# A decoder block on one core: FFN weight sums issued two pieces ahead of their splits, and the first rest product in another pair of banks

## The chip, the cores and the metric

The kernel runs on one core of a Trainium2 chip. The metric is device time in microseconds of one execution, the median of several runs. Five engines matter: TensorE (PE, with its weight loads PEld), VectorE (DVE), ScalarE (ACT), GpSimd (POOL, which here only issues DMAs) and SyncE (SP, which issues most loads).

## The reference

One decoder layer in float32 over 512 positions of width 2048: latent attention and stick-breaking attention, merged by sigmoid gates, and then a SwiGLU FFN of inner width 5632. Cut to the part that the change touches:

```python
h2 = _rms(x, g_norm2) * (1 + sc2) + sh2
gate, up = jnp.split(h2 @ w_ffn_in, 2, axis=-1)
x = x + gt2 * ((jax.nn.silu(gate) * up) @ w_ffn_out)
```

`w_ffn_in` is 2048 x 11264, `w_ffn_out` 5632 x 2048.

## The kernel before, in words

All large products are float32 made out of three products of rounded halves: a weight `raw` is cast by ACT to a rounded `whi` and DVE subtracts, `wlo = raw - whi`; TensorE then does `wlo`·x-high, `whi`·x-high and `whi`·x-low. Three buffers of `whi` and three of `wlo` turn round.

The FFN is the last part. Its two matrices are cut in 2 x 2 blocks (11, 12, 21, 22) and multiplied with 7 block products in place of 8 (the Winograd scheme), P1 to P7, each of which takes a sum of blocks of the weights and a sum of blocks of the activations. The first matrix is worked through in 11 column groups (`FG`). In each, a product is 4 pieces (j0 to j3), a piece is one 128 x 1024 weight tile and 12 matmuls of 128 x 512. Activation sums are named `x12` and `x34` with h and l for the halves.

Groups 0 to 3 (`NPRE`) begin early: their products E1 and E2 (`ffn_in_early`) come first for all four, in banks ps_s for even groups and ps_t for odd ones, and ACT empties the banks afterwards (`out`). The rest of an early group is R5, R7, R3, R6, R4; a full group has P1, P5, P6, P3, P7, P2, P4 (`ffn_in_group`). The groups follow one another in the order 0, 4, 1, 5, 2, 6, 3, 7, 8, 9, 10 (`seq`). A product accumulates in a bank pair that has a letter: A is ps_s, ps_s; B is ps_t, ps_t; C is ps_mm, ps_mm; D is ps_mm, ps_y. R5 and R3 share B. After each group the result goes through transposes back to rows (`act_back1`, `act_back2`), is summed (`s12`, `s34`), split (`y12h`, `y12l`, `y34h`, `y34l`, and a plain `x22`) and parked in device memory (`apark`) by DMAs that POOL issues. `act_back2` of a group runs in the next one: after R5 in a rest group, after P1 in a full one. The second matrix (`ffn_out_chunk`) is worked through in five chunks of groups, its operands `yb` coming back from `apark`; each product is added to `acc` by DVE.

The weights: `raw_load` lets SP load a 128 x 1024 block into one of ten buffers (`raw2`). Where a product needs a sum of weight blocks, that sum is made in place by DVE, `raw <- raw + raw`: the tuple behind the product's name in `PROD`, for R7 `("12", "12", "22")`, says that block 12 becomes the sum of 12 and 22 (the minus signs of the scheme lie in the sums of activations). Only P7's is made by an accumulating DMA that POOL issues (`piece_add`). What sets the order: every product adds its pieces to a list (`add_piece`), other steps go between them (`add_do`), and `run_ev` goes through the list; for each piece `ahead_to(i, 2, 6)` first issues loads six pieces ahead and makes the splits two pieces ahead. `piece_make` issues for one piece: its sum if it has one, the cast `whi` on ACT, the `wlo` on DVE. Some steps wait in the list `late` and are let out two per piece (`flush(2)`). What comes out is the program order; the tile scheduler then orders each engine's instructions anew by when it expects them to be ready, so the places below are taken from the built kernels.

All vector operations are issued through a helper, so that the profile has one line for them: L83 before, L84 after.

Of the kernel before, what the change touches and what calls it, by code (L numbers as in the profile page):

```python
# [14 lines left out]
ALU = mybir.AluOpType  # L15
# [4 lines left out]
D = 2048  # L20
# [12 lines left out]
NF = 20  # L33
HSTEP = 2
GF = (1, 1)
NPRE = 4


# [50 lines left out]
def kernel(  # L89
# [22 lines left out]
    vec, act, pe = Ordered(tc, nc.vector), Ordered(tc, nc.scalar), Ordered(tc, nc.tensor)  # L112
# [13 lines left out]
    def nm(s):  # L126
        uid[0] += 1
        return f"{s}_{uid[0]}"

    def t2(name, dtype=F32, w=T):  # L130
        return tp.tile([P, w], dtype, tag="t2", name=nm(name))
# [8 lines left out]
    def ps(tag, w=T):  # L140
        return pp.tile([P, w], F32, tag=tag, name=nm("ps_" + tag), bufs=PSB[tag])
# [141 lines left out]
    for k in range(KD):  # L283
        t = t2("xt")
# [517 lines left out]
    for hh in range(H):  # L802
# [5 lines left out]
        last = hh == H - 1  # L808
# [336 lines left out]
    raws = {}  # L1145
# [16 lines left out]
    def raw_load(key):  # L1162
        if key in raws:
            return
        r = st["rp2"].tile([P, 1024], F32, tag="raw2", name=nm("raw2"))
        src, km = raw_src(key)
        sync_dma(r.rearrange("p (a b) -> p a b", b=128 if km else 256), src)
        raws[key] = r

    def raw_add(key, onto):  # L1170

        src, km = raw_src(key)
        nc.gpsimd.dma_start(raws[onto].rearrange("p (a b) -> p a b", b=128 if km else 256), src,  # L1173
                            accum_op=ALU.add)

    def kmc(key, ap):

        if key[0] == "a" and key[1] == 0:
            return ap.rearrange("p (k m c) -> p k m c", k=2, m=4)
        return ap.rearrange("p (m k c) -> p k m c", k=2, m=4)  # L1180
# [3 lines left out]
    PROD = {  # L1184
# [7 lines left out]

# [13 lines left out]
    def piece_add(stage, g, prod, j):  # L1206
        if prod == "P7":
            raw_add((stage, g, "22", j), (stage, g, "T3", j))

    def piece_make(stage, g, prod, j):  # L1210
        _, sums_, blk, _, last = PROD[prod]
        rw = lambda b: raws[stage, g, b, j]
        for d, x, y in sums_:
            vec.tensor_tensor(rw(d), rw(x), rw(y), ALU.add)
        key, r = (stage, g, blk, j), rw(blk)
        hi = wp.tile([P, 1024], F32R, tag="whi", name=nm("whi"), bufs=3)
        lo = wp.tile([P, 1024], F32R, tag="wlo", name=nm("wlo"), bufs=3)
        v4 = lambda t: t.rearrange("p (k m c) -> p k m c", k=2, m=4)
        act.copy(v4(hi), kmc(key, r))
        vec.tensor_tensor(v4(lo), kmc(key, r), v4(hi).bitcast(F32), ALU.subtract)  # L1220
        for b in last:
            del raws[stage, g, b, j]
        return hi, lo

    ev = []
    made = {}
    cur = {"load": 0, "add": 0, "make": 0}
    pieces = []

    def add_piece(args, use):  # L1230
        pieces.append(args)
        ev.append((len(pieces) - 1, use))
# [4 lines left out]
    def ahead_to(i, n_make, n_load):  # L1237
        while cur["load"] < min(i + n_load + 1, len(pieces)) or cur["make"] < min(i + n_make + 1, len(pieces)):
            if cur["load"] <= cur["make"] or cur["load"] < min(i + n_load + 1, len(pieces)):
                stage, g, prod, j = pieces[cur["load"]]  # L1240
                for b in PROD[prod][3]:
                    raw_load((stage, g, b, j))
                cur["load"] += 1
            else:
                while cur["add"] < min(cur["make"] + 4, cur["load"]):
                    piece_add(*pieces[cur["add"]])
                    cur["add"] += 1
                made[cur["make"]] = piece_make(*pieces[cur["make"]])
                cur["make"] += 1

    late = []

# [4 lines left out]
    def run_ev():  # L1257
        for i, fn in ev:
            if i is None:
                fn()  # L1260
            else:
                ahead_to(i, 2, 6)
                fn(made.pop(i))
                flush(2)

    def ffn_begin():
        ahead_to(0, 0, 3)

    def prod_mm(bank, hl, w, kk, first, last):

        wh, wl = w
        cs = slice(kk * 512, kk * 512 + 512)
        xh, xl = hl[:2]
        for t in range(2):
            mm3(bank[t], (xh[:, t * P:(t + 1) * P], xl[:, t * P:(t + 1) * P]), (wh[:, cs], wl[:, cs]),
                first, last, skip_group_check=True)

    def tb(*tags):
        return [ps(t) for t in tags]
# [25 lines left out]
    def ffn_in_group(g, early, prev):  # L1305
        G = groups.setdefault(g, {})
        n = KD // 4
# [6 lines left out]
        def product(prod, bank, start, stop, js=range(KD // 4)):  # L1314
            def use(w, j):
                if j == 0 and start:
                    G[bank] = tb(*{"A": ("s", "s"), "B": ("t", "t"), "C": ("mm", "mm"), "D": ("mm", "y")}[bank])
                for kk in range(2):
                    prod_mm(G[bank], X[PROD[prod][0], 2 * j + kk], w, kk, start and j == 0 and kk == 0,
                            stop and j == n - 1 and kk == 1)  # L1320
            for j in js:
                add_piece(("a", g, prod, j), lambda w, j=j: use(w, j))
# [81 lines left out]
        else:  # L1404
# [11 lines left out]
            if g == FG - 1:  # L1416
# [8 lines left out]
    epark = {(g, i, t): dp.tile([P, T], F32, name=f"epark_{g}_{i}_{t}")  # L1425
             for g in range(1, NPRE) for i in range(2) for t in range(2)}
    apark = [dp.tile([P, 7 * T], F32, name=f"apark_{i}") for i in range(2 * FG)]
# [87 lines left out]
    def mark_banks():  # L1515

        for o in tb("mm", "mm", "mm", "y"):
            pe.matmul(o, onesr, X[(1, 1), 0][2], start=True, stop=True)
    for g in range(0, NPRE, 2):
        for i in range(2):  # L1520
            ffn_in_early(g, i)
            ffn_in_early(g + 1, i)
    seq = [g for p in zip(range(NPRE), range(NPRE, 2 * NPRE)) for g in p] + list(range(2 * NPRE, FG))
    for g, prev in zip(seq, [None] + seq):
        ffn_in_group(g, g < NPRE, prev)

# [218 lines left out]
```

## Time and profile before

| | us |
|---|---|
| median of 3 runs | 2638.85 |
| lowest, highest | 2637.84, 2639.08 |
| the profiled execution | 2637.33 |
| its span, first to last instruction | 2635.6 |
| PE busy | 2568.4 (97%) |
| DVE busy | 1933.1 (73%) |
| ACT busy | 1176.8 (45%) |
| POOL busy | 221.5 (8%) |
| mean granted TensorE clock | 0.998 |

The profiled execution is a little below the median of the runs and 1.7 us longer than its own span. PE is busy nearly all the time, so an edit shows where PE was idle, or where its clock was low; idle time of the other engines costs nothing by itself. Times in the text are microseconds from the start of the span. The products of the FFN begin near 1307 us.

### The profile page before, as it was taken

The page shows a single profiled execution, that of the slowest core. Times are in us where ns is not written, and L with a number is a line of the kernel's source. Part 1 is how long each engine was busy: PE and PEld are TensorE (multiplying, and loading weights), DVE is VectorE, ACT ScalarE, POOL GpSimd, SP SyncE. Part 2 cuts the span into 40 slices and gives each one's busy share as a digit, 9 for nine tenths or more (in the row PEclk, how much of TensorE's full clock was granted, in tenths as well). Part 3 has the DMA queues.
Part 4 walks back from the last instruction along what each step waited for, and adds up shares of the span by engine and source line. Part 5 has one row for each costly group of instructions (what it writes and reads, how often), then busy time and mean ns, then how long its engine had stood idle before and what let it go on. Part 6 is the DMA issues. An engine that isn't in the chain of part 4 may idle for free. (4 is left out here: it accounts for less than half of the span.)

```text
span 2635.6 us, 32539 instructions
## 1 busy us (share of the span) xinstructions
PE 2568.4 (97%) x12170; PEld 2139.3 (81%) x12170; DVE 1933.1 (73%) x2507; ACT 1176.8 (45%) x1613; POOL 221.5 (8%) x316
## 2 busy tenths in 40 slices
PE   6999999999999999999999999999999999999998
PEld 4788887888998888888887878787888888788887
DVE  8967766666788764543587788887977778678887
ACT  4435556642333322222384545454555555444442
POOL 0000000000001100000000212121211221000001
PEclk9999999999999999999999999999999999999999
DMA  9864444435666695343475767675877778888894
GB/s 340 291 221 133 175 156 126 140 126 223 260 258 232 244 340 209 128 158 142 130 221 168 203 201 208 199 223 178 252 200 203 213 228 323 247 251 239 262 285 144
DMA packets 309477, 558.62 MB, mean 212 GB/s; under 512 B 17924, under 2 KB 229636, under 8 KB 284232
## 3 DMA queue, kind: packets, MB, share of 16 engines
q1 hardware_dynamic: 263424, 471.13, 52.5%
q0 software_dynamic: 39840, 74.73, 10.9%
q10 hardware_dynamic: 6056, 10.70, 1.1%
q8 instruction: 95, 1.56, 0.2%
q14 instruction: 62, 0.51, 0.1%
HBM read 494.09 MB, written 62.39 MB: 211 GB/s over the span
## 5 line engine op out<-in xcount | busy, mean ns | idle before, releaser
L83 ACT CAST whi<-raw 128x1024 fp32r<-128x1024 f32 x672 | 704.2, 1050 | 974.2 <-PE ps_mm L83 488.4
L83 DVE TENSOR_TENSOR wlo<-raw,whi 128x1024 fp32r<-128x1024 f32 x672 | 816.9, 1218 | 366.1 <-ACT whi L83 356.3
L83 PE MATMUL ps_mm<-hl,whi 128*128 128x512 f32 x832 | 327.2, 393 | 0.0
L83 PE MATMUL ps_mm<-hh,whi 128*128 128x512 f32 x832 | 325.0, 391 | 0.0
L83 PE MATMUL ps_mm<-hh,wlo 128*128 128x512 f32 x832 | 324.8, 390 | 0.0
L83 DVE TENSOR_TENSOR raw<-raw,raw 128x1024 f32<-128x1024 f32 x218 | 264.5, 1220 | 29.3 <-DMA raw<-in_w_ff_dram 26.8
L272 DVE CUSTOM_DVE_ANT_0 raw<-raw,cb,cols 128x2048 f32<-128x2048 f32 x96 | 224.6, 2344 | 4.5 <-DMA raw<-in_w_ada_dram 4.5
L83 PEld LDWEIGHTS ps_mm<-hh,wlo 128*128 128x128 f32 x832 | 156.2, 188 | 32.5
L83 PEld LDWEIGHTS ps_mm<-hl,whi 128*128 128x128 f32 x832 | 156.5, 188 | 30.5
L83 PEld LDWEIGHTS ps_mm<-hh,whi 128*128 128x128 f32 x832 | 156.5, 188 | 30.4
L83 PE MATMUL ps_s<-whi,x 128*128 128x512 f32 x576 | 177.6, 390 | 0.0
L83 PE MATMUL ps_mm<-whi,yb 128*128 128x512 f32 x440 | 135.6, 389 | 0.0
L83 PEld LDWEIGHTS ps_s<-whi,x 128*128 128x128 f32 x576 | 108.2, 188 | 22.6 <-DVE x L83 0.2
L83 PE MATMUL ps_s<-wlo,x 128*128 128x512 f32 x288 | 113.1, 393 | 1.8 <-ACT x L83 1.8
L83 PE MATMUL ps_mm<-whi,x 128*128 128x512 f32 x352 | 108.5, 389 | 0.0
L83 PE MATMUL ps_s<-whi,yb 128*128 128x512 f32 x352 | 108.5, 390 | 0.0
L83 PE MATMUL ps_t<-whi,yb 128*128 128x512 f32 x352 | 108.4, 389 | 0.0
L83 PE MATMUL ps_mm<-mgl,whi 128*128 128x512 f32 (+1 forms) x272 | 102.7, 377 | 0.0
L83 PE MATMUL ps_mm<-mgh,whi 128*128 128x512 f32 (+1 forms) x272 | 102.4, 376 | 0.0
L83 PE MATMUL ps_mm<-mgh,wlo 128*128 128x512 f32 (+1 forms) x272 | 102.4, 376 | 0.0
L1173 POOL DMA_DIRECT2D raw<-in_w_ff_dram x46 | 58.3, 1268 | 458.9 <-DMA raw<-in_w_ff_dram 236.3
L83 PEld LDWEIGHTS ps_mm<-whi,yb 128*128 128x128 f32 x440 | 82.6, 188 | 16.9
(392 smaller groups left out, 5296.0 us busy)
## 6 DMA issues: line engine op xcount, KB each, us to landing
raw<-in_w_ff_dram SPq DMA_DIRECT2D x342, 512.0 KB, 4.8
raw<-in_w_ada_dram SPq DMA_DIRECT2D x96, 1024.0 KB, 5.0
yb<-apark SPq DMA_DIRECT2D x154, 256.0 KB, 6.4
raw<-in_w_gate_dram SPq DMA_DIRECT2D x27, 1024.0 KB, 4.9
raw<-in_w_sb_dram SPq DMA_DIRECT2D x24, 1024.0 KB, 4.8
raw<-in_w_ff_dram POOLq DMA_DIRECT2D x46, 512.0 KB, 8.2
raw<-in_w_out_dram SPq DMA_DIRECT2D x16, 1024.0 KB, 4.8
raw<-in_w_gate_dram SPq DMA_DIRECT2D x24, 512.0 KB, 4.3
```

What stands on the lines that cost most here:

```text
L83: ins = f(*a, **kw)
L272: tc.keep_in_program_order(nc.vector.tensor_tensor_reduce(raw, raw, cb, 1.0, col(C_B + 16 * ADA[name] + j), ALU.mult, ALU.add, dst))
L1173: nc.gpsimd.dma_start(raws[onto].rearrange("p (a b) -> p a b", b=128 if km else 256), src, accum_op=ALU.add)
```

## The change

Two things. The bank letter B is ps_s, ps_s in place of ps_t, ps_t for group 0 alone, which concerns its R5 and R3. And the in-place sums leave `piece_make`: a new counter `cur["sum"]` says up to which piece the sums are made; `sums_to` makes them up to a given piece, and stops where a sum would overwrite a block that an earlier piece still has to be split from. The sum of a piece is made at the latest just before its split, and after each split the sums are made up to the second piece behind it that has been loaded.

```diff
--- before.py
+++ after.py
@@ -33,6 +33,7 @@
 NF = 20
 HSTEP = 2
 GF = (1, 1)
+SUMS = 2
 NPRE = 4
 
 
@@ -1207,11 +1208,25 @@
         if prod == "P7":
             raw_add((stage, g, "22", j), (stage, g, "T3", j))
 
+    def piece_sum(stage, g, prod, j):
+        rw = lambda b: raws[stage, g, b, j]
+        for d, x, y in PROD[prod][1]:
+            vec.tensor_tensor(rw(d), rw(x), rw(y), ALU.add)
+
+    def sums_to(n):
+
+        while cur["sum"] < min(n + 1, cur["load"]):
+            stage, g, prod, j = pieces[cur["sum"]]
+            news = {(stage, g, d, j) for d, _, _ in PROD[prod][1]}
+            olds = {(s_, g_, PROD[p_][2], j_) for s_, g_, p_, j_ in pieces[cur["make"]:cur["sum"]]}
+            if news & olds:
+                return
+            piece_sum(stage, g, prod, j)
+            cur["sum"] += 1
+
     def piece_make(stage, g, prod, j):
-        _, sums_, blk, _, last = PROD[prod]
+        _, _, blk, _, last = PROD[prod]
         rw = lambda b: raws[stage, g, b, j]
-        for d, x, y in sums_:
-            vec.tensor_tensor(rw(d), rw(x), rw(y), ALU.add)
         key, r = (stage, g, blk, j), rw(blk)
         hi = wp.tile([P, 1024], F32R, tag="whi", name=nm("whi"), bufs=3)
         lo = wp.tile([P, 1024], F32R, tag="wlo", name=nm("wlo"), bufs=3)
@@ -1224,7 +1239,7 @@
 
     ev = []
     made = {}
-    cur = {"load": 0, "add": 0, "make": 0}
+    cur = {"load": 0, "add": 0, "make": 0, "sum": 0}
     pieces = []
 
     def add_piece(args, use):
@@ -1245,8 +1260,10 @@
                 while cur["add"] < min(cur["make"] + 4, cur["load"]):
                     piece_add(*pieces[cur["add"]])
                     cur["add"] += 1
+                sums_to(cur["make"])
                 made[cur["make"]] = piece_make(*pieces[cur["make"]])
                 cur["make"] += 1
+                sums_to(cur["make"] + SUMS - 1)
 
     late = []
 
@@ -1314,7 +1331,7 @@
         def product(prod, bank, start, stop, js=range(KD // 4)):
             def use(w, j):
                 if j == 0 and start:
-                    G[bank] = tb(*{"A": ("s", "s"), "B": ("t", "t"), "C": ("mm", "mm"), "D": ("mm", "y")}[bank])
+                    G[bank] = tb(*{"A": ("s", "s"), "B": ("s", "s") if g == 0 else ("t", "t"), "C": ("mm", "mm"), "D": ("mm", "y")}[bank])
                 for kk in range(2):
                     prod_mm(G[bank], X[PROD[prod][0], 2 * j + kk], w, kk, start and j == 0 and kk == 0,
                             stop and j == n - 1 and kk == 1)
```

On the chip's queues this reads as follows. In DVE's instructions 56 of the 218 sums stand in another place, 35 of them earlier. The first place is R7 of an early group, here group 2. `s` are the sums of the transposed results, `y12l` and `y34l` their splits, `raw_2455` is the block that R7's last piece j3 uses; the first `wlo` is that of j2, the last that of j3. Before:

```order
L83 TENSOR_TENSOR wlo_13940<-raw_2451_13724,whi_13939 128x1024
L83 SCALAR_TENSOR_TENSOR s_2492_13922<-y_2467_13813,s_2491_13921 128x256
L83 TENSOR_TENSOR s_2496_13932<-y_2494_13928 128x256
L83 TENSOR_TENSOR s_2497_13933<-y_2471_13826,y_2494_13928 128x256
L83 SCALAR_TENSOR_TENSOR s_2496_13932<-s_2496_13932,y_2471_13826 128x256
L83 TENSOR_TENSOR y12l_13962<-s_2491_13921,y12h_13961 128x512
L83 SCALAR_TENSOR_TENSOR s_2497_13933<-y_2471_13826,s_2496_13932 128x256
L83 TENSOR_TENSOR raw_2455_13745<-raw_2455_13745,raw_2479_13855 128x1024
L83 TENSOR_TENSOR y34l_13985<-s_2492_13922,y34h_13984 128x512
L83 TENSOR_TENSOR x_2495_13930<-y_2494_13928,x_2495_13930 128x256
L83 TENSOR_TENSOR y12l_14009<-s_2496_13932,y12h_14008 128x512
L83 TENSOR_TENSOR wlo_13969<-raw_2455_13745,whi_13968 128x1024
```

After:

```order
L84 TENSOR_TENSOR raw_2455_13747<-raw_2455_13747,raw_2479_13857 128x1024
L84 SCALAR_TENSOR_TENSOR s_2491_13923<-s_2491_13923,y_2467_13815 128x256
L84 TENSOR_TENSOR s_2492_13924<-y_2467_13815,y_2489_13919 128x256
L84 SCALAR_TENSOR_TENSOR s_2492_13924<-y_2467_13815,s_2491_13923 128x256
L84 TENSOR_TENSOR wlo_13941<-raw_2451_13726,whi_13940 128x1024
L84 TENSOR_TENSOR s_2496_13934<-y_2494_13930 128x256
L84 TENSOR_TENSOR s_2497_13935<-y_2471_13828,y_2494_13930 128x256
L84 SCALAR_TENSOR_TENSOR s_2496_13934<-s_2496_13934,y_2471_13828 128x256
L84 TENSOR_TENSOR wlo_13969<-raw_2455_13747,whi_13968 128x1024
```

The sum has moved up past j2's `wlo`, and j3's `wlo` has moved up past the `y12l` and `y34l` operations.

The second place is the step from P5 to P6 in a full group, here group 5. `raw_2330` and `raw_2334` are the blocks that P6's pieces j2 and j3 use; the `wlo` out of `raw_2325` is that of j1. Before:

```order
L83 TENSOR_TENSOR wlo_13366<-raw_2322_13042,whi_13365 128x1024
L83 TENSOR_TENSOR y12l_13382<-s_2374_13296,y12h_13381 128x512
L83 TENSOR_TENSOR x_2373_13294<-y_2372_13292,x_2373_13294 128x256
L83 TENSOR_TENSOR raw_2330_13086<-raw_2378_13306,raw_2330_13086 128x1024
L83 TENSOR_TENSOR y34l_13388<-s_2375_13297,y34h_13387 128x512
L83 TENSOR_TENSOR wlo_13395<-raw_2325_13061,whi_13394 128x1024
L83 TENSOR_TENSOR raw_2334_13108<-raw_2385_13337,raw_2334_13108 128x1024
```

After:

```order
L84 TENSOR_TENSOR x_2368_13285<-y_2367_13283,x_2368_13285 128x256
L84 TENSOR_TENSOR wlo_13367<-raw_2322_13044,whi_13366 128x1024
L84 TENSOR_TENSOR raw_2330_13088<-raw_2378_13308,raw_2330_13088 128x1024
L84 TENSOR_TENSOR y12l_13384<-s_2374_13298,y12h_13383 128x512
L84 TENSOR_TENSOR wlo_13396<-raw_2325_13063,whi_13395 128x1024
L84 TENSOR_TENSOR y34l_13390<-s_2375_13299,y34h_13389 128x512
L84 TENSOR_TENSOR raw_2334_13109<-raw_2385_13339,raw_2334_13109 128x1024
L84 TENSOR_TENSOR x_2373_13296<-y_2372_13294,x_2373_13296 128x256
```

Both sums have moved up by one or two small operations, and the two x operations now stand one before the first sum, one behind the second, while the `wlo` of j1 comes before the second y34l. ACT's casts and POOL's parkings of the same tiles follow in the same sense: the parking of the first x comes behind those of the first y12 and y34.

## Rows read from the trace of the kernel before

**Rows 1.** Waits of PE from 1380 us on: total us, times, longest us.

```profile
PE ps_mm L83 <- DVE wlo L83: 20.0, 12, 2.8
PE ps_t L83 <- ACT s L83: 4.1, 1, 4.1
```

**Rows 2.** Part 5 of the page: busy us, mean ns, idle before, releaser.

```profile
L83 DVE TENSOR_TENSOR wlo<-raw,whi 128x1024 fp32r<-128x1024 f32 x672 | 816.9, 1218 | 366.1 <-ACT whi L83 356.3
```

**Rows 3.** Timeline of PE: start, us, what, count, [idle before, releaser].

```profile
1400.63 0.50 PE L83 MATMUL ps_t<-wlo,x12h 128*128 128x512 f32 x1 [4.13 <-ACT s L83]
```

**Rows 4.** Stretches: busy us (x) of PE, PEld, DVE, ACT, POOL; PEclk, DMA, GB/s.

```profile
1401.40:1405.00 3.60, 3.60 (x10) 2.79 (x9) 0.90 (x1) 0.00 (x0) 0.54 (x2) 0.53 0.36 146
1844.90:1848.70 3.80, 3.72 (x9) 2.95 (x10) 2.90 (x4) 0.89 (x1) 2.08 (x4) 0.55 0.94 302
1405.00:1408.60 3.60, 3.60 (x17) 2.95 (x17) 1.22 (x1) 1.59 (x2) 0.00 (x0) 1.00 0.00 0
```

**Rows 5.** Timeline of PE in R7 of groups 1, 2 and 3.

```profile
1562.42 0.50 PE L83 MATMUL ps_mm<-wlo,x34h 128*128 128x512 f32 x1 [2.40 <-DVE wlo L83]
...
1703.75 0.50 PE L83 MATMUL ps_mm<-wlo,x34h 128*128 128x512 f32 x1 [2.72 <-DVE wlo L83]
...
1844.98 0.56 PE L83 MATMUL ps_mm<-wlo,x34h 128*128 128x512 f32 x1 [2.79 <-DVE wlo L83]
```

**Rows 6.** Timeline of PE in P6 of four full groups.

```profile
1485.11 0.50 PE L83 MATMUL ps_mm<-wlo,x12h 128*128 128x512 f32 x1 [1.20 <-DVE wlo L83]
...
1626.09 0.50 PE L83 MATMUL ps_mm<-wlo,x12h 128*128 128x512 f32 x1 [1.68 <-DVE wlo L83]
...
1766.37 0.50 PE L83 MATMUL ps_mm<-wlo,x12h 128*128 128x512 f32 x1 [0.61 <-DVE wlo L83]
...
1987.45 0.50 PE L83 MATMUL ps_mm<-wlo,x12h 128*128 128x512 f32 x1 [0.60 <-DVE wlo L83]
```

**Rows 7.** Timeline of PE in P4, the longest of three.

```profile
1815.52 0.50 PE L83 MATMUL ps_mm<-wlo,x 128*128 128x512 f32 x1 [2.62 <-DVE wlo L83]
```

**Rows 8.** Timeline of ACT at the end of the early products.

```profile
1390.81 1.07 ACT L83 ACTIVATE s<-ps_s 128x512 f32<-128x512 f32 x2
...
1399.99 1.08 ACT L83 ACTIVATE s<-ps_t 128x512 f32<-128x512 f32 x2
```

**Rows 9.** Timeline of DVE, the first wlo of R5 of group 0.

```profile
1395.47 1.22 DVE L83 TENSOR_TENSOR wlo<-raw,whi 128x1024 fp32r<-128x1024 f32 x1
```

**Rows 10.** Timeline of DVE in R7 of group 2.

```profile
1695.39 0.42 DVE L83 TENSOR_TENSOR s<-y 128x256 f32<-128x256 f32 x1
...
1696.39 1.22 DVE L83 TENSOR_TENSOR wlo<-raw,whi 128x1024 fp32r<-128x1024 f32 x1
...
1699.81 1.22 DVE L83 TENSOR_TENSOR raw<-raw,raw 128x1024 f32<-128x1024 f32 x1
...
1702.48 2.35 DVE L83 TENSOR_TENSOR wlo<-raw,whi 128x1024 fp32r<-128x1024 f32 x2
```

**Rows 11.** Timeline of SP there; SP's DMA issues, median us to landing.

```profile
1689.28 2.69 SPq L179 DMA_DIRECT2D raw<-in_w_ff_dram  x2
...
raw<-in_w_ff_dram SPq DMA_DIRECT2D x2, 512.0 KB, 4.4
```

**Rows 12.** Timeline of DVE between P5 and P6, second full group.

```profile
1622.13 0.69 DVE L83 TENSOR_TENSOR y12l<-s,y12h 128x512 fp32r<-128x512 f32 x1 [2.85 <-DMA apark<-x]
...
1624.82 1.22 DVE L83 TENSOR_TENSOR wlo<-raw,whi 128x1024 fp32r<-128x1024 f32 x1
```

**Rows 13.** DMA issues from 1604 to 1616 us, median us to landing.

```profile
raw<-in_w_ff_dram SPq DMA_DIRECT2D x2, 512.0 KB, 4.7
...
apark<-x POOLq DMA_DIRECT2D x1, 256.0 KB, 8.1
```

**Rows 14.** Timeline of SP in the same stretch.

```profile
1605.88 2.64 SPq L179 DMA_DIRECT2D raw<-in_w_ff_dram  x2
```

**Rows 15.** Timeline of DVE in P4, next group's sum.

```profile
1671.39 1.22 DVE L83 TENSOR_TENSOR raw<-raw,raw 128x1024 f32<-128x1024 f32 x1 [1.59 <-DMA raw<-in_w_ff_dram]
```

## The prediction

> **What bounds the kernel now.** The page comes first: TensorE (PE) is busy for 97% of the span, so only its idle time and its slow stretches can be won. Next comes the list of PE's waits from 1380 us on, where nearly all of the FFN lies: 20.0 us in 12 waits of a product in the mm banks for a DVE `wlo` (the split's remainder), and one wait of 4.1 us for an ACT copy out of ps_t [rows 1]. The groups of the page show why DVE is waited for though it is not full: a `wlo` takes 1218 ns, 672 of them fill 817 us, and what DVE idles before them is mostly for ACT's `whi` [rows 2]; it is single places where a `wlo` that TensorE needs stands behind something that waits for a DMA. The timelines then give four sorts of place.
>
> A. Once: the first product R5 of group 0 waits 4.13 us for ACT to empty ps_t of the last early product [rows 3]. After it the clock falls: in the 3.60 us from 1401.40 on PE has a granted clock of 0.53 and 10 matmuls, in the next 3.60 us of full clock 17 [rows 4].
> B. R7, last piece j3, of groups 1 to 3: 2.40, 2.72 and 2.79 us [rows 5]; the last is again followed by a stretch at a granted clock of 0.55, close to the 1.2 GHz level, with 9 matmuls in 3.80 us [rows 4].
> C. P6, second piece j1, in the full groups: 1.20, 1.68, 0.61 and 0.60 us [rows 6].
> D. The rest of the list: P4, third piece, three times (2.62 us the longest [rows 7]), and one place of FFN-out. That is 20.0 - 7.91 (B) - 4.09 (C) = 8.0 us for these and one wait of 0.3 us in R7 of group 0.
>
> **The change part by part.** No instruction is added or removed on any engine, and none of SP's loads is moved: the same 218 sums of 1.22 us, the same splits, the same transfers (POOL issues a few of its parkings in another order). So the sum is made from waits alone. 56 of the 218 sums change their place among DVE's instructions, 35 of them to an earlier one. The places that matter are three.
>
> *The bank (A).* R5 and R3 of group 0 now use the s banks. The products that filled them were emptied by two ACT copies that began at 1390.81 and took 1.07 us, 4.6 us before R5 could start; the copies out of ps_t that R5 waited for began only at 1399.99 [rows 8]. The next user of ps_s is P1 of group 4, the five products of this group later, so no wait appears behind it. What is late next is R5's own first `wlo`, 1395.47 + 1.22 = 1396.69 [rows 9]; PE was free at 1400.63 - 4.13 = 1396.50. So R5 starts near 1396.75 rather than 1400.63: 3.9 us. Without the long idle time I take it that the clock does not fall: 17 - 10 = 7 matmuls of 3.60/17 = 0.21 us, 1.5 us. Together **5.4 us**. The cost from below: if the clock falls all the same, 3.9.
>
> *R7 (B).* In the order after, the sum for j3 stands before the split of j2 and j3's `wlo` two and a half small operations behind that; before, the sum came late and two y12l, a y34l and an x stood between it and its `wlo`. Before, `wlo` of j2 began at 1696.39, the sum at 1699.81, the next `wlo` at 1702.48 [rows 10]. The sum's load is the second of two that SP issues between 1689.28 and 1691.97, with 4.4 us to landing [rows 11], so it lands near 1696. Replayed in the new order: sum 1695.85 to 1697.07, three s operations of 0.33 each (before, three of them fill the time from 1695.39 to 1696.39), `wlo` j2 from 1698.0 to 1699.2, three more s, `wlo` j3 from 1700.2 to 1701.4. PE needs j2 at about 1703.75 - 2.72 - 2.72 (one piece, 12 matmuls of 0.227) - 0.3 = 1698.0 and j3 one piece later. So j3 is ready and a wait of about 1.25 us appears at j2 in place of 2.72 at j3. For three groups: 7.91 - 3 x 1.25 = **4.2 us**. With no idle time of over 2.7 us left there, the slow stretch behind group 3's wait goes too, at the same price as above: **1.5 us**. Bounds: if the wait only moves, 0; if it goes wholly, 7.9 + 1.5.
>
> *P5 to P6 (C).* Before, the second y12l of the back transposes waited 2.85 us, from 1619.29 to 1622.13, for the parking of an x, and the `wlo` that P6 j1 needed began at 1624.82 [rows 12]. That parking goes out of POOL behind two accumulating loads and takes 8.1 us to land [rows 13]. After, the x operation and its parking stand later, the second y12l takes a buffer that is free from DVE's and ACT's own work, and the sum ahead of it needs the second of two loads of SP that were issued between 1605.88 and 1608.52 [rows 14], with 4.7 us to landing [rows 13]: it lands near 1613, six us early. So: `wlo` to 1619.3, sum to 1620.4, y12l to 1621.0, `wlo` of j1 to 1622.2, where PE wants it at 1626.09 - 1.68 - 0.3 = 1624.1. The whole wait goes: **4.1 us** for the four places. What is late next is ACT: its second y34h now waits for the parking of the second y12h (landing near 1622), and P6 j2's whi and `wlo` stand behind it: `wlo` near 1626.0 against a need of 1624.1 + 2.72 = 1626.8. The cover is 0.8 us there and, by the same replay, 0.25 us in the first full group. If it fails, one us comes back per place. Bounds: 0 to 4.1.
>
> *FFN-out and D.* 21 of the 35 moves pass one operation, and in FFN-out, with 14 of them, that is a 0.7 us accumulation out of a bank; neither the sum nor the accumulation is there what TensorE waits for. I take 0, and ±1 for the last chunk, where the output tiles wait for accumulations. D's rows are in the same order as before: a sum of the next group waits 1.59 us at 1671.39 for a load and holds the `wlo` of P4 [rows 15]. It stays.
>
> A rule that speaks against the change: at 1671.39 DVE did nothing for 1.59 us with a split standing behind the sum [rows 15]. The Trainium skill (Perfetto Trace Analysis, section "Tensor Engine Instruction (MATMUL, LD_WEIGHTS)") says that DVE, ACT and GpSimd execute strictly first in, first out, so every sum that is put ahead of a split can hold it for its load; by that rule sums made earlier cost time wherever a load is not early, which is the second rival below. The row agrees with the rule; whether it bites at the new places depends on the loads.
>
> **Sum:** 5.4 + 4.2 + 1.5 + 4.1 = 15.2 us. The profiled execution is 2637.33 us (span 2635.6 and 1.7 around it), so 2622.1 for it; the median of the runs shown is 1.5 us above the profiled one, so 2638.85 - 15.2 = **2623.6 us**.
>
> **The rivals.**
> 1. Only the bank pays: R7's wait moves to j2 with its whole price, since j2's `wlo` stands behind one more sum, and C's wait re-forms at ACT's y34h, which now waits for a parking. For: the covers of 0.25 and 0.8 us are thin, and j2 does become late. Against: the work of DVE between is the same and one long DMA wait leaves it. Time: 2638.85 - 5.4 = 2633.4.
> 2. Slower, by one mechanism: sums moved ahead of a split wait for their loads as in D. Places: three in R7 and two in each of the seven full groups at P5 to P6, 17 in all. At D's price of 1.59 us [rows 15] that is 27 us, B and C win nothing, the bank still gives 5.4: 2638.85 + 27 - 5.4 = 2660.4. It decides from 5.4/17 = 0.32 us of waiting per sum on. Against it: the six us by which the load is early in C; for it: in R7 the load lands just when the sum wants it [rows 11].
> 3. DVE has no slack behind A: the wait of 0.3 us at group 0's R7 shows `wlo` just in time there, and PE arriving 5.4 us earlier would only wait longer at the next splits; C and B as in rival 1. Time: between 2635 and 2639, not to be told from before.
> 4. More: D goes as well, because the loads behind it are issued when splits free their buffers, and those come earlier. 2638.85 - 15.2 - 5.3 (of the 8.0 of D all but 0.3 in R7 and 2.4 in FFN-out) = 2618.3.
>
> **How the numbers follow.** A measurement of this kernel can tell about 0.2%, 5.3 us, from no change: the limits are 2633.6 and 2644.1. The forecast, with its sizes between 2619 and 2629: 0.60. Rival 1: 0.20, of which 0.12 end below 2633.6 and 0.08 above. Rival 2: 0.05. Rival 3: 0.07. Rival 4: 0.08. So faster 0.60 + 0.12 + 0.08 = 0.80, same 0.08 + 0.07 = 0.15, slower 0.05. The range goes from 2616 (rival 4, the 1 us of the last chunk, and another for waits of under 0.3 us that no row shows) to 2634 (rival 1), which leaves out rivals 2 and 3 and the upper part of rival 1.
>
> **What would show it.** PE's wait for ACT `s` in ps_t is gone and R5 begins in ps_s behind a wait of under 0.5 us for a `wlo`; no stretch near 1400 or 1840 has a granted clock near 0.5; R7 of groups 1 to 3 shows a wait of 1 to 1.5 us one piece earlier, none at j3; the four waits at P6 j1 are gone, and none of over 0.3 us is at P6 j2; the P4 waits are still there; the list's 20.0 us fall to about 12. It would be wrong if PE's time is the same and the waits stand elsewhere (rival 3), if DVE's idle time before sums, now mostly for loads, grows by more than 5 us (rival 2), or if R7's wait has the old size one piece earlier (rival 1).

## The result, and the profile after

The changed kernel takes 2624.39 us (median of 4 runs, 2621.63 to 2626.18) against 2638.97 us for the kernel before (2637.84 to 2639.77): a ratio of 0.9937, 95% interval 0.992 to 0.9954, that is 14.6 us less by the medians and 16.6 by the ratio, whose interval (12.1 to 21.1) holds both. The forecast was 2623.6. The profiled execution took 2622.97 us with a span of 2621.2, 14.4 less than the span before; its mean granted clock is 0.998, as in the profiled execution before.

The list of PE's waits from 1380 us on, with the same columns as [rows 1]. The line of 4.1 us for ACT is gone; a wait of 0.5 us for a `wlo` in ps_s is there in its place, and 20.0 us in 12 waits have become 10.3 in 8:

```profile
PE ps_mm L84 <- DVE wlo L84: 10.3, 8, 2.4
...
PE ps_s L84 <- DVE wlo L84: 0.5, 1, 0.5
```

The timeline of PE shows the places, with start, duration and, in brackets, the idle time before and what ended it. The first line is R5 of group 0, in ps_s now [rows 3]; 1555.96, 1693.34 and 1830.84 are R7 of groups 1 to 3 [rows 5]; 1620.50 is P6's piece j1 in the second full group, without a bracket, so without a wait [rows 6]; 1530.09, 1668.20 and 1805.50 are P4's third piece [rows 7]:

```profile
1399.86 0.47 PE L84 MATMUL ps_s<-wlo,x12h 128*128 128x512 f32 x1 [0.50 <-DVE wlo L84]
...
1530.09 0.50 PE L84 MATMUL ps_mm<-wlo,x 128*128 128x512 f32 x1 [2.27 <-DVE wlo L84]
...
1555.96 0.50 PE L84 MATMUL ps_mm<-wlo,x34h 128*128 128x512 f32 x1 [0.35 <-DVE wlo L84]
...
1620.50 0.39 PE L84 MATMUL ps_mm<-wlo,x12h 128*128 128x512 f32 x1
...
1668.20 0.50 PE L84 MATMUL ps_mm<-wlo,x 128*128 128x512 f32 x1 [1.29 <-DVE wlo L84]
...
1693.34 0.50 PE L84 MATMUL ps_mm<-wlo,x34h 128*128 128x512 f32 x1 [1.04 <-DVE wlo L84]
...
1805.50 0.50 PE L84 MATMUL ps_mm<-wlo,x 128*128 128x512 f32 x1 [1.21 <-DVE wlo L84]
...
1830.84 0.50 PE L84 MATMUL ps_mm<-wlo,x34h 128*128 128x512 f32 x1 [1.42 <-DVE wlo L84]
```

| place | idle before, us | idle after, us |
|---|---|---|
| A: R5 of group 0 | 4.13 | 0.50 |
| B: R7 of groups 1 to 3 | 2.40 + 2.72 + 2.79 | 0.35 + 1.04 + 1.42 |
| C: P6, second piece | 1.20 + 1.68 + 0.61 + 0.60 | none |
| D: P4, third piece | 5.3 | 2.27 + 1.29 + 1.21 |
| FFN-out, second chunk | 2.4 | 2.4 |

On DVE the two stretches of the prediction look like this. First the step from P5 to P6 [rows 12]: the sum, the second y12l without its wait of 2.85 us, and the `wlo` of j1. Then R7 of group 2 [rows 10]: the sum that waits 0.24 us for its load, `wlo` of j2, `wlo` of j3:

```profile
1615.46 1.22 DVE L84 TENSOR_TENSOR raw<-raw,raw 128x1024 f32<-128x1024 f32 x1
1616.59 0.69 DVE L84 TENSOR_TENSOR y12l<-s,y12h 128x512 fp32r<-128x512 f32 x1
1617.19 1.22 DVE L84 TENSOR_TENSOR wlo<-raw,whi 128x1024 fp32r<-128x1024 f32 x1
...
1689.91 1.23 DVE L84 TENSOR_TENSOR raw<-raw,raw 128x1024 f32<-128x1024 f32 x1 [0.24 <-DMA raw<-in_w_ff_dram]
...
1692.06 1.22 DVE L84 TENSOR_TENSOR wlo<-raw,whi 128x1024 fp32r<-128x1024 f32 x1
...
1694.21 1.22 DVE L84 TENSOR_TENSOR wlo<-raw,whi 128x1024 fp32r<-128x1024 f32 x1
```

In R7 the replay had the two `wlo` 2.2 us apart, and so they are (1692.06 and 1694.21); PE waited 1.04 us at j2 and not at j3.

On DVE as a whole, the idle time before the sums (the last columns of these lines of part 5 of the page, before and after) hardly changed:

```profile
L83 DVE TENSOR_TENSOR raw<-raw,raw 128x1024 f32<-128x1024 f32 x218 | 264.5, 1220 | 29.3 <-DMA raw<-in_w_ff_dram 26.8
...
L84 DVE TENSOR_TENSOR raw<-raw,raw 128x1024 f32<-128x1024 f32 x218 | 265.0, 1221 | 30.2 <-DMA raw<-in_w_ff_dram 27.7
```

The stretches, with the columns of [rows 4], hold the one thing that went another way. The slow stretch behind A is gone (last line, 18 matmuls at full clock), but this execution has three others that the profile of the kernel before does not have: near 401 and 1310 us, where the two programs are the same, and behind the P4 wait at 1530:

```profile
400.80:403.90 3.10, 3.10 (x9) 2.43 (x9) 2.31 (x6) 0.63 (x1) 0.00 (x0) 0.51 0.71 288
1309.50:1312.00 2.50, 2.50 (x7) 1.96 (x6) 2.50 (x6) 2.50 (x8) 0.00 (x0) 0.50 0.00 0
1530.40:1533.80 3.40, 3.40 (x10) 2.64 (x9) 3.09 (x4) 0.00 (x0) 0.00 (x0) 0.54 0.56 171
1401.40:1405.00 3.60, 3.60 (x18) 2.96 (x17) 3.60 (x6) 2.77 (x5) 1.07 (x2) 1.00 0.00 0
```

### The profile page after: what moved, and what is told of

It reads as the page before. It is cut to its first block, busy times and chain, and to the rows that moved or that the text cites. A ratio compares the mean times of both kernels' runs of the same rounds, so it can differ in the third digit from the quotient of the medians.

```text
span 2621.2 us, 32537 instructions
## 1 busy us (share of the span) xinstructions
PE 2567.8 (98%) x12170; PEld 2140.6 (82%) x12170; DVE 1932.6 (74%) x2507; ACT 1175.8 (45%) x1613; POOL 221.5 (8%) x316
## 4 chain that ended last, share of the span: by engine, by line
PE 88%; DVE 5%; DMA 4%; issue 1%; ACT 1%; SPq 0%; DVEq 0%; ACTq 0%; POOLq 0%
PE ps_mm L84 55%; PE ps_t L84 14%; PE ps_s L84 13%; PE ps_y L84 6%; DMA raw<-in_w_ff_dram 3%; DVE wlo L84 2%; DVE raw L273 1%; DVE raw L84 1%; ACT whi L84 1%; DMA xo<-xpark 0%; DMA raw<-in_w_ada_dram 0%; DMA xt<-in_xT_dram 0%; DMA gpark<-sg 0%; DVE silu L84 0%; DVE hl L84 0%
## 5 line engine op out<-in xcount | busy, mean ns | idle before, releaser
L84 DVE TENSOR_TENSOR raw<-raw,raw 128x1024 f32<-128x1024 f32 x218 | 265.0, 1221 | 30.2 <-DMA raw<-in_w_ff_dram 27.7
```

The source lines that it names most:

```text
L84: ins = f(*a, **kw)
```

## The experiments

All ratios are to the kernel before, run on the same chip; times of different batches differ by some us in that kernel too (its medians lie between 2638.97 and 2642.49), so the ratios are what is compared. One per cent is 26.4 us, and where a text below says how many us less a kernel takes than the kernel before, that is worked out from its ratio. The intervals are ±0.0010 to ±0.0017, which is ±2.6 to ±4.5 us.

**The four parts of the change.** The changed kernel's instructions on DVE, ACT, POOL and PE differ from those of the kernel before at two sets of places that do not overlap: the bank alone touches the matmuls and copies of R5 and R3 of group 0, the sums alone all the rest. So the two halves can be run apart, and the sums again in two parts.

The bank alone:

```diff
-"B": ("t", "t")
+"B": ("s", "s") if g == 0 else ("t", "t")
```

> The kernel before with the bank of R5 and R3 of group 0 changed, sums as before. Theory (the parts of the change add up): the wait of 4.1 us for ACT in ps_t goes, a wait of about 0.5 us for a wlo stays, and the slow stretch behind it goes; the waits of R7 (2.4 to 2.8 us, groups 1 to 3) and of P6 (1.2, 1.7, 0.6, 0.6) stand as before: 5 us less than before, about 2634. Rival (DVE has no slack behind): the later waits grow by what R5 gains, time within 2 us of before, 2637 or more.

Measured: 2636.18 us, ratio 0.9979 (0.9969 to 0.9989), 5.5 us less. The list of PE's waits:

```profile
PE ps_mm L83 <- DVE wlo L83: 15.5, 11, 3.0
```

The wait for ACT is gone, and R5 of group 0 starts with none that the list shows. R7 still waits 2.3, 1.9 and 3.0 us, P6 0.5, 0.7 and 1.8. The bank's price in the prediction, 5.4, lies well within the interval (2.9 to 8.2), and rival 3 (no slack behind A) falls: the later waits did not grow in sum. The one profile is not a check of the price's two terms, however. DVE's order is that of the kernel before, and still P4's three waits make 2.8 us in place of 5.3 and P6's 3.0 in place of 4.1, while six slow stretches stand in it in place of two. The sizes of such waits and the number of slow stretches vary from one profile to the next.

The sums alone are the changed kernel with the old pair for B:

```diff
-"B": ("s", "s") if g == 0 else ("t", "t")
+"B": ("t", "t")
```

> The changed kernel with R5 and R3 of group 0 in the old ps_t pair: the sums alone. Theory: the 4.1 us wait stays, R7 of groups 1 to 3 waits 0.3 to 1.5 us one piece earlier in place of 2.4 to 2.8, P6's four waits are gone: 10 us less than before (8 to 12), about 2629. Rival (only the bank pays): within 2 us of before, with the waits at other pieces.

Measured: 2629.75 us, ratio 0.9954 (0.9942 to 0.9967), 12.1 us less. The list keeps the wait for ACT and loses 7.7 us of the rest (6.9 with the 0.9 and 0.3 us for splits in the ps_t and ps_s banks); P6's four waits are gone, and R7 waits 1.6, 1.6 and 0.3 us:

```profile
PE ps_mm L84 <- DVE wlo L84: 12.3, 9, 2.6
PE ps_t L84 <- ACT s L84: 4.4, 1, 4.4
```

Bank and sums together make 5.5 + 12.1 = 17.6, and the whole change, measured twice, made 16.6 and 17.7 by its ratios (0.9937 and, below, 0.9933): they add up within the intervals.

Only the sums of the early groups' rest, or only those of the full groups and FFN-out; the others stay where their split is made:

```diff
-    def sums_to(n):
+    def sums_to(n, only=None):
...
+            if only and prod not in only:
+                return
...
-                sums_to(cur["make"] + SUMS - 1)
+                sums_to(cur["make"] + SUMS - 1, ("R5", "R7", "R3", "R6", "R4"))
```

> The changed kernel, but only the sums of R5, R7 and R6 products are made ahead; those of the full groups and of FFN-out stand as before. Theory: bank and R7 together, P6's waits (1.2 to 1.7 and 0.6 us) back: 10 us less than before (8 to 12), about 2629. Rival (R7's gain is an effect of the work in the full groups, or is lost there): 5 us less, like the bank alone.

Measured: 2625.93 us, ratio 0.9940 (0.9927 to 0.9952), 15.8 us less, more than expected and nearly as much as the whole change. R7 waits 1.0, 1.2 and 0.5 us. Of the waits at P6 only the first came back, on PE's timeline:

```profile
1481.23 0.50 PE L84 MATMUL ps_mm<-wlo,x12h 128*128 128x512 f32 x1 [1.08 <-DVE wlo L84]
```

In the second full group DVE's second y12l did not wait, although no sum there had moved: the x operation stands in front of it as before, but behind the first y34l,

```profile
1612.56 0.41 DVE L84 TENSOR_TENSOR x<-y,x 128x256 fp32r<-128x256 f32 x1
...
1614.03 0.68 DVE L84 TENSOR_TENSOR y12l<-s,y12h 128x512 fp32r<-128x512 f32 x1
```

and on POOL the parking of that x goes out behind those of the first y12 and y34, not ahead of them:

```profile
1613.19 0.72 POOL L1455 DMA_DIRECT2D apark<-y34l  x1
1613.90 0.55 POOL L1501 DMA_DIRECT2D apark<-x  x1
```

So three of the four waits of C go without P6's own sums, on which the prediction had its eye. The bank alone left them, so it is the early groups' sums: once these stand in another order, the scheduler also places the x operation of the full group that follows later, and the second y12l does not wait for its parking. Which of the early groups' sums does it was not tried.

The other half, with the products' names P1 to P4 in the diff's last line:

> The changed kernel, but only the sums of the full groups and FFN-out are made ahead; R7's sum stands as before. Theory: bank and P6 together, R7's waits of 2.4 to 2.8 us back at the last piece: 10.5 us less than before (8 to 12), about 2628.5. Rival (the wait re-forms at the second y34h): 5 us less, with waits of over 0.5 us at P6 j2.

Measured: 2629.71 us, ratio 0.9954 (0.9941 to 0.9966), 12.1 us less, of which the bank makes 5.5. No wait of over 0.2 us is at P6; R7 still waits 2.7, 1.7 and 2.9 us, and this is most of what is left:

```profile
PE ps_mm L84 <- DVE wlo L84: 13.7, 7, 2.9
```

Either half of the sums thus removes most of C, which is one reason why 15.8 + 12.1 - 5.5 = 22.4 is more than the whole change brought; the shared waits are about 3 us of the 5 between, and the rest is within the intervals.

**The changed kernel again, and what the clock does.** No edit.

> The changed kernel once more, beside the three that follow. Theory: the waits for wlo at P4 (D) and the lesser ones at R7 stand where they stood, their sizes within 1 us; the stretches at half clock are drawn anew in each execution behind one or other of the longer waits, so their places differ from those of the first profile (400, 1309 and 1530 us). Rival (a slow stretch belongs to a certain wait): the same three places.

Measured: 2623.41 us (2620.46 to 2628.18), ratio 0.9933 (0.9920 to 0.9947). The waits at P4 in the second and third place are 1.88 and 2.66 us where the first profile had 1.29 and 1.21, the one in the first place is gone and R5 behind it waits 1.07 instead. The sizes differ by up to 2.3 us though DVE's order is the same in both profiles; "within 1 us" was too narrow. The slow stretches are others. In these rows (with the columns of [rows 4]) the first two places, which had granted clocks of 0.51 and 0.50 in the first profile, are at full clock, and three other places are slow:

```profile
400.80:403.90 3.10, 3.10 (x15) 2.53 (x14) 2.88 (x6) 0.86 (x2) 0.00 (x0) 1.00 0.60 241
1309.50:1312.00 2.50, 2.50 (x12) 2.06 (x11) 2.50 (x7) 2.50 (x7) 0.00 (x0) 1.00 0.26 75
1664.40:1667.80 3.40, 3.40 (x9) 2.61 (x8) 3.19 (x4) 0.00 (x0) 0.00 (x0) 0.51 0.65 194
1804.20:1807.60 3.40, 3.40 (x10) 2.68 (x9) 3.08 (x3) 0.08 (x1) 0.00 (x0) 0.53 0.68 218
2279.00:2281.90 2.90, 2.90 (x8) 2.30 (x7) 2.39 (x3) 0.73 (x2) 0.00 (x0) 0.50 0.00 0
```

The rival in its strict form falls: no wait brings a slow stretch each time. Some places return more often than others, though: the 2.4 us wait in FFN-out is followed by one in six of the nine profiles that have it. By the starts of its matmuls, 427 ns apart in place of 227, each of the three costs 1.5 to 1.6 us, as each of the three in the first profile does.

**Other orders of the sums.** Sums four pieces ahead:

```diff
-SUMS = 2
+SUMS = 4
```

> The changed kernel with sums up to four pieces ahead of their splits rather than two. Theory (a sum ahead of a split costs only where its load is late): the loads are issued six pieces ahead, about 16 us, and take 5 us, so most sums still find theirs, some not: DVE's idle time before sums grows by up to 8 us, the time is 0 to 5 us above the changed kernel. Rival (earlier is better without limit): below the changed kernel by 2 us or more. Rival 2 of the prediction (every sum moved waits): 15 us or more above.

Measured: 2629.18 us, ratio 0.9951 (0.9938 to 0.9963), 5.8 us above the changed kernel on the same chip, so at the upper end of the 0 to 5 that were expected, given the intervals, and nowhere near 15; "earlier is better" falls. But the reason was wrong. DVE's idle time before sums hardly grew. From 1380 us on it is 30.7 us with four ahead, against 29.2 with two in the run above:

```profile
L84 DVE TENSOR_TENSOR raw<-raw,raw 128x1024 f32<-128x1024 f32 x217 | 263.6, 1221 | 30.7 <-DMA raw<-in_w_ff_dram 28.1
```

What grew are PE's waits in new places, in the ps_t and ps_s banks. With four ahead:

```profile
PE ps_mm L84 <- DVE wlo L84: 8.5, 7, 2.4
PE ps_t L84 <- DVE wlo L84: 3.5, 5, 0.9
PE ps_s L84 <- DVE wlo L84: 2.1, 3, 1.0
```

with two ahead:

```profile
PE ps_mm L84 <- DVE wlo L84: 9.3, 6, 2.7
...
PE ps_t L84 <- DVE wlo L84: 1.2, 2, 1.1
...
PE ps_s L84 <- DVE wlo L84: 0.5, 2, 0.3
```

11.0 us became 14.1. A sum takes 1.22 us of DVE away from the split that it passes, whether or not its load is there: in R3 of group 1, where TensorE now waits 0.91 us, two sums stand ahead of the split (from 1560.70 and 1564.18 us). That this makes all of the 5.8 us is not shown.

All sums and splits kept in program order (`keep` ties an instruction to the one kept before it on its engine):

```diff
+    def keep(ins):
+        return ins if vec.on else tc.keep_in_program_order(ins)
...
-            vec.tensor_tensor(rw(d), rw(x), rw(y), ALU.add)
+            keep(vec.tensor_tensor(rw(d), rw(x), rw(y), ALU.add))
...
-        vec.tensor_tensor(v4(lo), kmc(key, r), v4(hi).bitcast(F32), ALU.subtract)
+        keep(vec.tensor_tensor(v4(lo), kmc(key, r), v4(hi).bitcast(F32), ALU.subtract))
```

> The changed kernel with sums and splits of the weights kept on DVE in the order in which the program issues them; the scheduler may move only the other operations between them. Theory (what is left in D and FFN-out is a split that the scheduler put behind a sum whose load is late, or behind an accumulation that waits for TensorE): the waits at P4 (1.2 to 2.3 us, three) and the one of 2.4 us in FFN-out go, and R7's of 1.0 to 1.4 us; about 9 us less than the changed kernel, 2615. Rival (DVE has no slack there, the splits come late whichever way): within 3 us of the changed kernel. Second rival (kept order holds splits behind sums that wait for loads): slower than the changed kernel by 3 us or more.

Measured: 2670.41 us, ratio 1.0108 (1.0094 to 1.0122), 47 us above the changed kernel. DVE's idle time before sums fell,

```profile
L84 DVE TENSOR_TENSOR raw<-raw,raw 128x1024 f32<-128x1024 f32 x218 | 265.6, 1218 | 10.3 <-DMA raw<-in_w_ff_dram 9.2
```

and no wait of over 0.2 us is left at P4 or at the place in FFN-out: as far as that the theory held. But many others came in:

```profile
PE ps_mm L84 <- DVE wlo L84: 14.5, 15, 3.5
PE ps_t L84 <- DVE wlo L84: 10.5, 10, 2.9
PE ps_s L84 <- DVE wlo L84: 8.3, 7, 3.5
```

and 35 of the 47 us are lost by 1496 us (the same matmul stands at 1461 in the first profile of the changed kernel), in the early products and R7 of group 0, where the normalised activations are made by DVE between the splits: kept in order, the splits come in bunches behind operations that wait for ACT. Here three come together, and TensorE starts at 1379.54 us, after a wait of 3.5 us for the first of them:

```profile
1377.66 0.69 DVE L84 TENSOR_TENSOR x34l<-s,x34h 128x512 fp32r<-128x512 f32 x1 [1.35 <-ACT x34h L84]
1378.27 3.49 DVE L84 TENSOR_TENSOR wlo<-raw,whi 128x1024 fp32r<-128x1024 f32 x3
```

Slow stretches add to it: this profile has seven, two of them of double length, and five of the seven lie between 1310 and 1454 us. The second rival had the sign, not the reason.

The same with `SUMS = 0`, each sum just ahead of its own split:

> As the kernel with kept order, but with each sum just ahead of its own split (nothing made ahead). It tells whether the kept order or the distance pays. Theory (what matters is that no split stands behind something late; a sum just ahead of its split is 1.22 us on that split's way): between the changed kernel and the kept order with two ahead, about 2620. Rival (the distance alone pays): 2630 or more, near the bank alone.

Measured: 2769.01 us, ratio 1.0482 (1.0468 to 1.0496), far above what either the theory or the rival named:

```profile
PE ps_mm L84 <- DVE wlo L84: 52.7, 76, 1.9
PE ps_t L84 <- DVE wlo L84: 42.0, 34, 2.8
```

With a fixed order the distance between sum and split is worth 99 us, and with the scheduler free, 12. This suggests that most of what making sums ahead could bring the scheduler had already taken in the kernel before.

**Two small pieces of order, in place of all.** `keep` gets a condition. First only P4's splits in groups 4 to 6 and the sums of the next group's R5:

```diff
+            keep(prod == "R5" and g > 0, vec.tensor_tensor(rw(d), rw(x), rw(y), ALU.add))
...
+        keep(prod == "P4" and stage == "a" and g < 2 * NPRE - 1, vec.tensor_tensor(v4(lo), kmc(key, r), v4(hi).bitcast(F32), ALU.subtract))
```

> The changed kernel, where only the splits of P4 in groups 4 to 6 and the sums of the next group's R5 are kept in program order, so that no sum that waits for its load stands ahead of the split that P4's third piece needs. Theory (D is a split behind a late sum, and only that): the three waits at P4, 4.8 to 5.7 us together in the two profiles of the changed kernel, go; R5 behind them begins with a wait of at most 0.5 us; 4 to 6 us less than the changed kernel, about 2619 (0.9915 of the kernel before). Rival (the loads are late and R5's splits wait in P4's place): within 1.5 us of the changed kernel, with waits of over 1 us in R5.

Measured: 2614.00 us, ratio 0.9904 (0.9890 to 0.9917). That is 0.9933 - 0.9904 = 0.0029 or 7.7 us below the changed kernel, with an uncertainty of about 5 us that also holds the 4 to 6 expected. The waits at P4 are gone and none came in R5: 11.0 us of waits for `wlo` became 7.1. This profile has no slow stretch, where the two of the changed kernel have three each, so about half of the difference in time may be clock. On DVE at the second of the three places the split stands ahead of the sum that waits for its load, which now waits alone [rows 15]:

```profile
1659.52 1.22 DVE L84 TENSOR_TENSOR wlo<-raw,whi 128x1024 fp32r<-128x1024 f32 x1
...
1663.25 1.22 DVE L84 TENSOR_TENSOR raw<-raw,raw 128x1024 f32<-128x1024 f32 x1 [1.38 <-DMA raw<-in_w_ff_dram]
```

Then only the second chunk of FFN-out. In the profiles before and after, the first of two accumulations out of P5's bank, which waited 2.92 us for P5's last matmul, and a sum stood ahead of the split of P6's first piece:

```diff
-                    vec.tensor_tensor(a, a, B[b][t], ALU.add)
+                    keep(ci == 1 and name == "22" and b == "B", vec.tensor_tensor(a, a, B[b][t], ALU.add))
```

with P6's sums and splits of that chunk kept likewise.

> The changed kernel, where in the second chunk of FFN-out the sums and splits of P6 and the two accumulations out of the bank of P5 are kept in program order: the accumulations, which wait for P5's last matmul, now stand behind the split that P6's first piece needs. Theory: the wait of 2.4 us near 2275 goes and with it, in the executions where it is followed by one, a slow stretch of 1.4 to 1.6 us; 2.4 to 4 us less than the changed kernel, about 2621 (0.992 of the kernel before). Rival (the wait moves to P6's second piece): within 1 us.

Measured: 2619.62 us, ratio 0.9931 (0.9917 to 0.9945). The wait of 2.4 us is gone from its place and none came at P6's second piece. But the list as a whole did not get shorter:

```profile
PE ps_mm L84 <- DVE wlo L84: 9.2, 7, 2.2
PE ps_s L84 <- DVE wlo L84: 2.2, 2, 1.3
...
PE ps_t L84 <- DVE wlo L84: 1.1, 2, 0.9
```

These are 12.5 us, against 11.0 in each profile of the changed kernel: P4's three waits, which this edit does not touch, make 5.7 us here, and R5 of group 0 waits 1.25. And the ratio differs by 0.0002 from the changed kernel's with intervals of ±0.0014. So it is shown that this wait goes, and not shown by this run that time is won.

Both:

> Both kept orders, of P4 with R5 and of P6 in FFN-out, on top of the changed kernel. Theory (they add up): 7 to 9 us less than the changed kernel, about 2616 (0.990 of the kernel before). Rival: no better than the better of the two alone.

Measured: 2611.72 us, ratio 0.9898 (0.9884 to 0.9911), 27 us below the kernel before and 9 below the changed one, as expected. It is 2.3 us below P4's order alone, the size of the wait in FFN-out, but the intervals of the two overlap. What is left of the waits for `wlo`:

```profile
PE ps_mm L84 <- DVE wlo L84: 3.5, 4, 1.5
...
PE ps_s L84 <- DVE wlo L84: 0.7, 1, 0.7
```

Last, on top of both, R7's last sum not ahead of the split of j2:

```diff
-            if news & olds:
+            if news & olds or prod == "R7" and j == 3 and cur["sum"] > cur["make"]:
                 return
```

> The kernel with both kept orders, where in addition the sum of R7's last piece is not made ahead: the scheduler then puts it right behind the split of j2 and the split of j3 five small operations later. Theory (in R7 of groups 1 to 3 DVE has about 1 us more work than time, in whichever order): by the replay of the prediction the split of j2 ends 1.2 us earlier and that of j3 near the time that TensorE wants it plus 1 us, so a wait of 0.5 to 1.3 us stands at j3 in place of that at j2; the time is within 1.5 us of the kernel with both orders (0.9898 of the kernel before). Rival (the remaining wait is only the sum's place ahead of j2's split): no wait of over 0.3 us in R7 of groups 1 to 3, 3 us less.

Measured: 2610.37 us, ratio 0.9888 (0.9872 to 0.9905), within the 1.5 us. The waits stand at j3, as the theory said, but are smaller than those at j2 were (0.16, 0.82 and 0.39 us in place of 1.52, 0.51 and 1.23):

```profile
PE ps_mm L84 <- DVE wlo L84: 1.5, 4, 0.8
```

So of R7's rest one part is the sum's place and one part DVE's work. In time the two kernels cannot be told apart.

## Why the prediction was right

*The bank.* Forecast 5.4 us, of which 3.9 for the wait and 1.5 for the clock. The bank alone brought 5.5, with an interval of 2.9 to 8.2. R5 began behind a wait of 0.50 us rather than the 0.25 of the sum, in other executions 0.3 to 1.25. Where the 4 us wait is gone and the scheduler is free, no slow stretch stands at this place, but as a term of one execution's sum the 1.5 us were not sound: see below.

*R7.* Forecast: a wait of 1.25 us at j2 in place of 2.4 to 2.8 at j3, 4.2 us. It was 0.35, 1.04 and 1.42 at j2, that is 7.91 - 2.81 = 5.1 us. The replay of DVE's order was made for group 2 and is 0.2 us off there, and its risk, a sum that finds its load just landing, cost 0.24 us. That it came so close has some luck in it: with the same order, group 2 waited 0.29 us in the second profile.

*P5 to P6.* Forecast 4.1 us, and all four waits went. "After, the x operation and its parking stand later, the second y12l takes a buffer that is free" was so, but the sums of P6 are not needed for it: three of the four waits also go when only the early groups' sums move, and all four when only those of the full groups and FFN-out do. The reordered output of the scheduler was read rightly, and what in the edit brought it about was not seen.

*D and FFN-out.* Forecast unchanged; D went from 5.3 to 4.8, in the second profile to 4.5 and 1.07 in R5 behind it, and FFN-out's 2.4 stayed 2.4. The row for D named the true cause, a split behind a sum that waits for its load, as the kept order of those few instructions showed: the whole wait went.

*The clock.* This is the term of the sum that was wrongly made. It had 1.5 us for each of the two slow stretches that the profile of before showed, 3.0 together. Both went from their places, but the profile after has three others. By the starts of their matmuls, 427 ns apart in place of 227, the two cost 3.1 us and the three 4.7. So the 14.4 us of the spans are 13.8 of waits and about 2 of small losses behind them, less about 1.6 of clock, where the forecast had 12.2 and 3.0. Of the waits, C came as priced, A 0.3 us short, B 0.9 better, and the rest are D's 0.5 and small ones. So the total came out close because a clock term 4.6 us too high was met by waits and restarts 3.6 us too low: that is luck.

For the mean over executions the term was not too high. The granted clocks of the runs tell this, profiled or not: the 40 runs of the kernel before beside the experiments had 0.994 to 0.997, mean 0.9958, none as high as the 0.998 of its profile; the nine of the changed kernel had 0.997 to 0.999, mean 0.9978. A profile with 0.996 (the bank alone) has six slow stretches, one with 0.998 (the changed kernel) three. By this estimate the change saves some three stretches, 4 to 5 us, in the mean, and the profile of before caught an execution with few of them. The term should have been such a mean, with its own range.

*The rivals.* "Only the bank pays" falls with the sums alone (12.1 us). "Sums wait for their loads" falls: DVE's idle time before sums went from 29.3 to 30.2 us, where the rival needed more than 5 us. At D, where the order had not been changed, the split stands behind a sum that waits for its load in both profiles. The Trainium skill's rule that DVE runs strictly first in, first out (Perfetto Trace Analysis, section "Tensor Engine Instruction (MATMUL, LD_WEIGHTS)") agrees with that, and with the two profiles of the changed kernel, whose DVE instructions stand in the same order from first to last. "D goes as well" did not happen.

## What to carry to other kernels

When one engine is near full, list its waits with what stands ahead of the awaited instruction on the releasing engine; each can be priced by replaying the new order with the durations of the old trace, and a few instructions held in place (P4's splits ahead of the next group's sums) bring more than fixing the order of all of them, which cost 47 us here. A sum or any preparation made earlier is worth something only up to the point where it passes a split that is wanted sooner. When a scheduler sets the order, look for the effect of an edit also where the edit is not. And price from more than one trace: with DVE's order unchanged, P4's three waits made 5.3 us in one profile and 2.8 in another, and a slow stretch in one trace is a chance and not a fixed cost.

## What the runs showed of the hardware that was not expected

TensorE's granted clock falls to the lower level, 1.2 GHz, behind some of its idle times and not behind others, in one execution here and in the next there. The wait of 1.8 us for ACT at the beginning of the FFN, near 1308 us, is in every kernel; a slow stretch followed it in 7 of the 14 profiles. In three, one stands near 2580 us behind four waits of only 0.3 to 0.9 us close together. Most stretches cost 1.4 to 1.7 us (by matmuls 427 ns apart in place of 227), and a profile had between none and six of them outside the kept-order kernels, not counting the one at the very end. The Trainium skill (TensorE: Matmul & The Clock Gate, section "What's actually happening") says that the clock is gated by how busy the engine has been; the rows agree that the stretches stand behind idle time, and show that which idle time it is cannot be read from one execution.

Roughly, fewer waits go with a higher mean clock over the runs. With 27 us of waits of PE from 1380 us on (the kernel before) it is 0.9958, with 19 (the bank alone) 0.9966, with 14 (the changed kernel) 0.9978, with 10 (P4's order) 0.9992, and with 100 (kept order, each sum beside its split) 0.9925. The times spread less, too: five runs of the changed kernel lie 7.7 us apart, four of the kernel with P4's order 2.1. So a wait that is removed seems to pay a second time, by slow stretches that do not come; most of the kernels fit that, not all (sums four ahead: 17 us and 0.9982), and no run changes the clock alone.
